# A dilated 3x3 convolution: the first pair stored whole between the halves of the fifth load, and the rows for four DMA engines taken from the second load

## The chip, the core and the metric

The kernel runs on one core of one Trainium2 chip. A core has a matrix engine (PE, with PEld for its weight loads), a vector engine (DVE), a scalar engine (ACT), a general engine (POOL) and a sequencer (SP) that computes nothing and issues the transfers here. Sixteen DMA engines move the data between the device memory (HBM) and the on-chip memory (SBUF). The metric is the device time of one execution in microseconds (us); the median over several executions is compared.

## What is computed

The input `x` has 16 images of 64 channels of 64 x 64 float32 values, `weight` is 128 x 64 x 3 x 3, the dilation is 2, and the output is 16 x 128 x 64 x 64 float32. Cut to what matters:

```python
pad = dilated_k // 2          # 2
x_pad = np.pad(x, ((0, 0), (0, 0), (pad, pad), (pad, pad)), mode='constant')
for b, co, ci, kh, kw in ...:
    output[b, co] += weight[co, ci, kh, kw] * \
        x_pad[b, ci, kh*dilation:kh*dilation+h, kw*dilation:kw*dilation+w]
```

Read once and written once, `x` is 16.8 MB and the output 33.6 MB.

## The kernel before

**Tiling.** Two images make a pair: their 2 x 64 channels fill the 128 partitions, so `x32` of one pair is a tile of 128 partitions by 4096 float32 (16 KB a partition, 2 MiB in all). There are eight pairs (0 to 7). A pair is worked on in four groups of 16 image rows, 32 groups `G` in all; `g` is the group within its pair. The output tile of a pair, `osb`, holds 128 output channels by two images, 32 KB a partition, 4 MiB in all; the two images are stored by separate calls, `store(pb, 0)` and `store(pb, 1)`, 2 MiB each.

**One group.** ACT casts rows of `x32` to float16 (`cast`, line 73), DVE adds pairs of rows (`rowsum`, line 85), PE forms three sets of products in PSUM, `psP`, `psA` and `psB` (line 171), ACT copies `psP` to SBUF as `p_sb` (line 227), and DVE adds `p_sb` to `psA` and to `psB` into the output tile (line 234). A group's last step is the second of these additions. The casts run ahead of the products: after the copy of group 0 three chunks have been cast, and each later group casts two more until it is far enough ahead. Chunks 0 to 3 belong to pair 0, chunks 4 to 7 to pair 1.

**Order.** The schedule is written out by hand: each engine executes its instructions in the order in which the code emits them. Every load and store is issued by SP, on one DMA queue, in program order; a transfer that has to wait for a tile holds up all that SP issues after it.

**Loads.** `x32` has three buffers (`XF = 3`). Pairs 0, 1 and 2 are loaded at the top (lines 89 to 91), pair 0 in two pieces. `load(3)` follows group 0 in the code and waits until the casts have read the whole of pair 0; pair 4 takes the buffer of pair 1 and so waits for chunk 7. In the kernel before, `load(4)` ("the fifth load", `load(XF + 1)`) comes after the stores of group 3. Pairs 5, 6 and 7 are loaded ahead of the stores of pairs 1, 2 and 3 (lines 243 and 244).

**Stores.** Pairs 1 to 6 are stored after their last group, 2 MiB a transfer. Pairs 0 and 7 are stored in halves, after their groups 1 and 3, 1 MiB a transfer. In pair 7 one of these, `store(7, 1)` of the first 32 rows, is cut further: 24 rows of all 128 partitions, and 8 rows (`ROWS4`) in two parts, partitions 0 to 123 and partitions 124 to 127 (`FOUR`). A row of eight image rows is 2 KB in one partition.

```python
FOUR = ((0, P - 4), (P - 4, P))
ROWS4 = 8
```

Of the kernel before, what the change touches and what calls it, by code (L numbers as in the profile page):

```python
# [10 lines left out]
def kernel(  # L11
# [7 lines left out]
    nc = tc.nc  # L19

    B, CI, H, W = x.shape
# [5 lines left out]
    d = 2  # L27

    P = 128
    f32 = mybir.dt.float32  # L30
# [4 lines left out]
    HW = H * W  # L35
    GR = 16
    NG = H // GR
    NBLK = GR // 4
    NH = GR // 2 * W
    npairs = B // 2  # L40
    ngroups = npairs * NG
    chunk_rows = [(g * GR + (d if g else 0), min((g + 1) * GR + d, H)) for g in range(NG)]
    XF = 3

    wpool = ctx.enter_context(tc.tile_pool(name="wpool", bufs=1))
    fpool = ctx.enter_context(tc.tile_pool(name="fpool", bufs=XF))
# [7 lines left out]
    x_pair = x.rearrange("(nb two) c h w -> nb (two c) (h w)", two=2)  # L54
    out_img = out.rearrange("b o h w -> b o (h w)")
# [2 lines left out]

    x32_tiles, x16_tiles, xs_tiles, o_tiles = {}, {}, {}, {}

    def load(pb, cuts=(0, H)):
        x32_tiles[pb] = fpool.tile([P, HW], f32, tag="x32", name="x32")
        for lo, hi in zip(cuts[:-1], cuts[1:]):
            nc.sync.dma_start(
                out=x32_tiles[pb][:, lo * W : hi * W], in_=x_pair[pb, :, lo * W : hi * W]
            )

    def cast(c):
        pb, g = divmod(c, NG)
# [7 lines left out]
    def rowsum(c):  # L77
        pb, g = divmod(c, NG)
        if g == 0:
            xs_tiles[pb] = sxpool.tile([P, HW // 2], f16, tag="xs", name="xs")  # L80
        v = x16_tiles[pb][:, g * GR * W : (g + 1) * GR * W].rearrange(
            "p (b e q) -> p b e q", e=2, q=2 * W
        )
        s = xs_tiles[pb][:, g * NH : (g + 1) * NH].rearrange("p (b q) -> p b q", q=2 * W)
        nc.vector.tensor_tensor(out=s, in0=v[:, :, 0], in1=v[:, :, 1], op=add)  # L85

    w32 = wpool.tile([CO, CI * KH * KW], f32, name="w32")
    nc.sync.dma_start(out=w32, in_=weight.rearrange("o i h w -> o (i h w)"))
    load(0, (0, 2 * GR + d, H))
    load(1)  # L90
    load(2)
    zero = wpool.tile([P, 512], f16, name="zero")
    nc.vector.memset(zero, 0.0)  # L93
# [25 lines left out]
    def turn(k):  # L119
# [24 lines left out]
        out=x16_tiles[0][:, 8 * W : 18 * W], in_=x32_tiles[0][:, 8 * W : 18 * W]  # L144
# [8 lines left out]
    def casts(G):  # L153
        for n in range(2 if G else 3):
            c = ahead[0]
            if c >= ngroups or c > G + (7 if c < 2 * NG else 5):
                return
            cast(c)
            ahead[0] += 1

    def product(ps, src, kind, blk0, nblk, first, last):
        for j in (1, 0, 2):
            dw = (j - 1) * d
            o0, o1 = max(0, -dw), W - max(0, dw)
            t = kind * KW + j
            for hb in range(2):
                pp = slice(hb * CI, (hb + 1) * CI)
                rhs = src(pp, dw + o0, dw + o1)
                po = ps[:, hb * NH + blk0 * 2 * W : hb * NH + (blk0 + nblk) * 2 * W]
                po = po.rearrange("p (r w) -> p r w", w=W)[:, :, o0:o1]  # L170
                nc.tensor.matmul(  # L171
                    out=po,
                    lhsT=w_sb[pp, t * CO : (t + 1) * CO],
                    rhs=rhs,
                    start=first and j == 1,
                    stop=last and j == 2,
                )

    def blocks(x16, b0, n, e):
        v = x16.rearrange("p (b e r w) -> p b e r w", e=2, r=2, w=W)  # L180
        return lambda pp, c0, c1: v[pp, b0 : b0 + n, e, :, c0:c1]

    def store(pb, m, r0=0, r1=H, rows=((0, P),)):
        for lo, hi in rows:
            nc.sync.dma_start(
                out=out_img[2 * pb + m, lo:hi, r0 * W : r1 * W],
                in_=o_tiles[pb][lo:hi, m * HW + r0 * W : m * HW + r1 * W],
            )

    FOUR = ((0, P - 4), (P - 4, P))  # L190
    ROWS4 = 8

    for G in range(ngroups):
        pb, g = divmod(G, NG)
        x16 = x16_tiles[pb]
        xs = xs_tiles[pb].rearrange("p (r w) -> p r w", w=W)
        if g == 0:
            o_tiles[pb] = opool.tile([P, 2 * HW], f32, tag="osb", name="osb")
        o = o_tiles[pb].rearrange("p (m b e q) -> p m b e q", m=2, e=2, q=2 * W)
        b0 = g * NBLK  # L200

        def summed():
            ps = ppool.tile([P, 2 * NH], f32, tag="p", name="psP")
            sv = lambda pp, c0, c1: xs[pp, g * GR // 2 : (g + 1) * GR // 2, c0:c1]
            product(ps, sv, 0, 0, NBLK, True, True)
            return ps

        if G:
            psP = summed()

        psA = apool.tile([P, 2 * NH], f32, tag="ab", name="psA")
        product(psA, blocks(x16, b0, NBLK, 1), 1, 0, NBLK, True, False)
        z = 1 if g == 0 else 0
        product(psA, blocks(x16, b0 + z - 1, NBLK - z, 1), 2, z, NBLK - z, False, True)

        psB = apool.tile([P, 2 * NH], f32, tag="ab", name="psB")
        product(psB, blocks(x16, b0, NBLK, 0), 3, 0, NBLK, True, False)
        z = 1 if g == NG - 1 else 0
        product(psB, blocks(x16, b0 + 1, NBLK - z, 0), 4, 0, NBLK - z, False, True)

        if not G:
            psP = summed()

        if not G:
            casts(0)
        p_sb = spool.tile([P, 2 * NH], f32, tag="psb", name="p_sb")
        nc.scalar.copy(out=p_sb, in_=psP)  # L227
        if G:
            casts(G)
        if G + 1 < ngroups:  # L230
            rowsum(G + 1)
        pv = p_sb.rearrange("p (m b q) -> p m b q", m=2, q=2 * W)
        for e, ps in ((0, psA), (1, psB)):
            nc.vector.tensor_tensor(  # L234
                out=o[:, :, b0 : b0 + NBLK, e],
                in0=ps.rearrange("p (m b q) -> p m b q", m=2, q=2 * W),
                in1=pv,
                op=add,
            )

        if G == 0:
            load(XF)
        if g == NG - 1 and 0 < pb < npairs - XF - 1:
            load(pb + XF + 1)
        if pb in (0, npairs - 1):
            if g % 2 == 1:
                store(pb, 0, (g - 1) * GR, (g + 1) * GR)
                if pb and g == 1:
                    store(pb, 1, 0, 2 * GR - ROWS4)
                    store(pb, 1, 2 * GR - ROWS4, 2 * GR, FOUR)  # L250
                else:
                    store(pb, 1, (g - 1) * GR, (g + 1) * GR)
            if G == NG - 1:
                load(XF + 1)
        elif g == NG - 1:
            store(pb, 0)
            store(pb, 1)

# [34 lines left out]
```

## Time and profile before

| what | value |
|---|---|
| median of 14 executions (lowest to highest) | 126.95 us (126.58 to 127.2) |
| the profiled execution: its own time | 126.99 us |
| its span in the profile | 125.2 us |
| PE busy in the span | 107.0 us (85%) |
| DVE busy | 90.9 us (73%) |
| ACT busy | 65.0 us (52%) |
| bytes moved by DMA | 50.78 MB |

The span is the part of the execution that the profile resolves, from the first to the last recorded instruction; 1.79 us of the profiled execution's own time lie around it. Times in the profile count from the start of the span. In the page's second part the span is cut into 40 slices of 3.13 us, a digit for each: 9 means busy for 90% of the slice or more. The DMA digit is a mean over the sixteen engines. A DMA has a time of issue, when SP executes the instruction, and a time of landing, when its last byte is reported.

### The profile page before, as it was taken

Reading aid. Unit: us, or ns where it says so; the run is one execution under the profiler, and the core shown is the slowest. Engines: PE = TensorE matmul, PEld = TensorE weight load, DVE = VectorE, ACT = ScalarE, POOL = GpSimd, SP = SyncE. Lnnn points to the kernel's source line nnn. Section 1 sums busy time; section 2 is a strip of 40 time slices with the busy share of each in tenths; the row PEclk is TensorE's granted clock in tenths of the full one; section 3 lists DMA queues with packets and bytes.
Section 4 is the critical chain, followed back from the end, with each engine's and each line's share of the span. In section 5 each row is a group of like instructions: output and inputs, shape, how many; then the busy total and the mean of one; then the engine's idle time right before and its main releaser. Section 6 shows DMA issues by size and latency. Waiting matters only on the chain.

```text
span 125.2 us, 2339 instructions
## 1 busy us (share of the span) xinstructions
PE 107.0 (85%) x1000; PEld 57.2 (46%) x1000; DVE 90.9 (73%) x103; ACT 65.0 (52%) x68; POOL 2.2 (2%) x8
## 2 busy tenths in 40 slices
PE   6899699999999999999999999999999999900000
PEld 2344355555555556555555555555555555500000
DVE  0560698988898888988988898889888988740000
ACT  4185798666566656665666566566653333300000
POOL 2400000000000000000000000000000000000000
PEclk9999999999999999999999999999999999995555
DMA  4999999899999999999999999999999999999991
GB/s 114 380 443 440 445 424 408 304 432 427 437 432 434 429 424 424 440 416 419 424 445 427 424 434 419 424 429 440 429 424 434 414 434 429 445 395 416 424 385 55
DMA packets 4466, 50.78 MB, mean 406 GB/s; under 512 B 488, under 2 KB 488, under 8 KB 1000
## 3 DMA queue, kind: packets, MB, share of 16 engines
q1 hardware_dynamic: 4456, 50.63, 96.5%
q8 instruction: 8, 0.13, 0.4%
q14 instruction: 2, 0.02, 0.0%
HBM read 17.07 MB, written 33.55 MB: 404 GB/s over the span
## 4 chain that ended last, share of the span: by engine, by line
PE 82%; DMA 2%; DVE 1%; DVEq 1%; ACT 1%; issue 0%
PE psA L171 32%; PE psB L171 31%; PE psP L171 16%; DMA w<-in_weight_dram 2%; PE wt L124 2%; PE dm L101 2%; DVE osb L234 1%; DVEq L290 1%; ACT p_sb L227 1%; DVE wd L111 0%; DVEq L234 0%
## 5 line engine op out<-in xcount | busy, mean ns | idle before, releaser
L171 PEld LDWEIGHTS <-w_sb 64*128 64x128 f16 x960 | 54.6, 95 | 46.7 <-issue 2.3
L227 ACT COPY p_sb<-psP 128x1024 f32<-128x1024 f32 x32 | 32.4, 1013 | 38.5 <-issue 21.5
L234 DVE TENSOR_TENSOR osb<-psA,p_sb 128x1024 f32<-128x1024 f32 x32 | 39.2, 1225 | 14.8 <-PE psA L171 9.4
L171 PE MATMUL psA<-x,w_sb 64*128 64x496 f16 (+3 forms) x384 | 45.9, 370 | 0.0
L171 PE MATMUL psB<-x,w_sb 64*128 64x496 f16 (+3 forms) x384 | 45.1, 365 | 0.0
L234 DVE TENSOR_TENSOR osb<-psB,p_sb 128x1024 f32<-128x1024 f32 x32 | 39.1, 1222 | 0.0
L73 ACT CAST x<-x 128x1024 f16<-128x1024 f32 (+2 forms) x31 | 32.1, 1046 | 0.0
L171 PE MATMUL psP<-xs,w_sb 64*128 64x496 f16 (+1 forms) x192 | 26.0, 371 | 1.1 <-ACT p_sb L227 1.1
L85 DVE TENSOR_TENSOR xs<-x 128x512 f16<-128x512 f16 x32 | 13.3, 416 | 0.2 <-ACT x L73 0.2
L101 PE MATMUL dm<-zero 128*128 128x512 f16 x10 | 5.0, 622 | 1.2 <-DVE zero L93 1.2
L124 PEld LDWEIGHTS <-wd 128*64 128x64 f16 x30 | 1.5, 162 | 2.5 <-DVE wd L111 1.3
L124 PE MATMUL wt<-ident,wd 128*64 128x128 f16 x30 | 2.2, 314 | 0.4 <-DVE wd L111 0.4
L111 DVE CAST wd<-w 128x192 f16<-128x192 f32 x1 | 0.5, 495 | 2.6 <-DMA w<-in_weight_dram 2.6
L101 PEld LDWEIGHTS <-zero 128*128 128x128 f16 x10 | 1.1, 124 | 2.8 <-issue 1.6
L113 ACT ACT_TABLE_LOAD x1 | 1.3, 1283 | 0.7 <-PEq L276 0.7
L136 ACT CAST w_sb<-wt 128x384 f16<-128x384 f32 x1 | 0.5, 480 | 2.0 <-PE wt L124 2.0
L113 ACT CAST wd<-w 128x192 f16<-128x192 f32 x1 | 0.5, 537 | 1.7 <-DMA w<-in_weight_dram 1.7
L138 DVE CAST w_sb<-wt 128x384 f16<-128x384 f32 x1 | 0.6, 557 | 1.2 <-PE wt L124 1.2
L93 DVE MEMSET zero<- 128x256 uint32 x1 | 0.3, 272 | 0.9 <-PEq L276 0.9
L148 DVE CAST w_sb<-wt 128x384 f16<-128x384 f32 x1 | 0.6, 558 | 0.4 <-PE wt L124 0.4
L112 POOL TENSOR_TENSOR wd<-w 128x192 f16<-128x192 f32 x1 | 0.8, 794 | 2.5 <-DMA w<-in_weight_dram 2.5
L115 POOL CAST wd<-w 128x192 f16<-128x192 f32 x1 | 0.8, 808 | 0.0
(11 smaller groups left out, 3.8 us busy)
## 6 DMA issues: line engine op xcount, KB each, us to landing
out_dram<-osb SPq DMA_DIRECT2D x12, 2048.0 KB, 17.4
x<-in_x_dram SPq DMA_DIRECT2D x7, 2048.0 KB, 15.4
out_dram<-osb SPq DMA_DIRECT2D x7, 1024.0 KB, 11.3
x<-in_x_dram SPq DMA_DIRECT2D x1, 1088.0 KB, 5.5
x<-in_x_dram SPq DMA_DIRECT2D x1, 960.0 KB, 7.3
out_dram<-osb SPq DMA_DIRECT2D x1, 768.0 KB, 14.4
w<-in_weight_dram SPq DMA_DIRECT2D x1, 288.0 KB, 3.0
out_dram<-osb SPq DMA_DIRECT2D x1, 248.0 KB
```

Of the source, the lines that this page charges most:

```text
L73: nc.scalar.copy(out=x16_tiles[pb][:, lo * W : hi * W], in_=x32_tiles[pb][:, lo * W : hi * W])
L85: nc.vector.tensor_tensor(out=s, in0=v[:, :, 0], in1=v[:, :, 1], op=add)
L101: nc.tensor.matmul(out=dm[:, 0:512], lhsT=zero[:, 0:P], rhs=zero)
L112: nc.gpsimd.tensor_tensor(out=wdv[:, 3], in0=wv[:, 0], in1=wv[:, 1], op=sub)
L113: nc.scalar.copy(out=wdv[:, 2], in_=wv[:, 0])
L115: nc.gpsimd.tensor_copy(out=wdv[:, 4], in_=wv[:, 2])
L124: nc.tensor.matmul(out=wts[k % 3][r * CI : (r + 1) * CI, c0 + j * CO : c0 + (j + 1) * CO], lhsT=wd[:, t * CI : (t + 1) * CI], rhs=ident,)
L138: nc.vector.tensor_copy(out=t2[0], in_=t2[1])
L171: nc.tensor.matmul(out=po, lhsT=w_sb[pp, t * CO : (t + 1) * CO], rhs=rhs, start=first and j == 1, stop=last and j == 2,)
L227: nc.scalar.copy(out=p_sb, in_=psP)
L234: nc.vector.tensor_tensor(out=o[:, :, b0 : b0 + NBLK, e], in0=ps.rearrange("p (m b q) -> p m b q", m=2, q=2 * W), in1=pv, op=add,)
L290: with _tile.TileContext(nc) as tc:
```

## The change

Five edits, all in the order and the cutting of transfers; no instruction of PE, DVE, ACT or POOL is changed.

1. Pair 0 is no longer stored in halves: `store(0, 0)` and `store(0, 1)` are issued once, after group 3, 2 MiB each.
2. `load(4)` is cut into two halves of 32 image rows. The first is issued after group 2, ahead of the stores of pair 0, the second after them.
3. `load(1)` is cut into 56 rows of all partitions, and 8 rows in two parts, partitions 0 to 123 and 124 to 127.
4. The store of the first half of image 1 of pair 7 is no longer cut: 1 MiB in one transfer.
5. `load(7)` is cut into two halves, issued one after the other where it stood.

```diff
-    def load(pb, cuts=(0, H)):
-        x32_tiles[pb] = fpool.tile([P, HW], f32, tag="x32", name="x32")
-        for lo, hi in zip(cuts[:-1], cuts[1:]):
...
+    ALL = ((0, P),)
+    FOUR = ((0, P - 4), (P - 4, P))
+    ROWS4 = 8
+
+    def load(pb, *pieces):
+        if pb not in x32_tiles:
+            x32_tiles[pb] = fpool.tile([P, HW], f32, tag="x32", name="x32")
+        for r0, r1, parts in pieces or ((0, H, ALL),):
+            for lo, hi in parts:
+                nc.sync.dma_start(
+                    out=x32_tiles[pb][lo:hi, r0 * W : r1 * W],
+                    in_=x_pair[pb, lo:hi, r0 * W : r1 * W],
+                )
...
-    load(0, (0, 2 * GR + d, H))
-    load(1)
+    load(0, (0, 2 * GR + d, ALL), (2 * GR + d, H, ALL))
+    load(1, (0, H - ROWS4, ALL), (H - ROWS4, H, FOUR))
     load(2)
...
         if G == 0:
             load(XF)
+        if G == NG - 2:
+            load(XF + 1, (0, H // 2, ALL))
         if g == NG - 1 and 0 < pb < npairs - XF - 1:
-            load(pb + XF + 1)
-        if pb in (0, npairs - 1):
+            load(pb + XF + 1, *((0, H, ALL),) if pb < 3 else ((0, H // 2, ALL), (H // 2, H, ALL)))
+        if pb == npairs - 1:
             if g % 2 == 1:
                 store(pb, 0, (g - 1) * GR, (g + 1) * GR)
-                if pb and g == 1:
-                    store(pb, 1, 0, 2 * GR - ROWS4)
-                    store(pb, 1, 2 * GR - ROWS4, 2 * GR, FOUR)
-                else:
-                    store(pb, 1, (g - 1) * GR, (g + 1) * GR)
-            if G == NG - 1:
-                load(XF + 1)
+                store(pb, 1, (g - 1) * GR, (g + 1) * GR)
         elif g == NG - 1:
             store(pb, 0)
             store(pb, 1)
+            if not pb:
+                load(XF + 1, (H // 2, H, ALL))
```

More of the change, by code (lines that the diff above doesn't have):

```diff
@@ L59 @@
     x32_tiles, x16_tiles, xs_tiles, o_tiles = {}, {}, {}, {}
-    def load(pb, cuts=(0, H)):
-        x32_tiles[pb] = fpool.tile([P, HW], f32, tag="x32", name="x32")
-        for lo, hi in zip(cuts[:-1], cuts[1:]):
-            nc.sync.dma_start(
-                out=x32_tiles[pb][:, lo * W : hi * W], in_=x_pair[pb, :, lo * W : hi * W]
-            )
+    ALL = ((0, P),)
[10 more added lines that the diff above has]
+                )
     def cast(c):
@@ L181, in blocks, with store @@
         return lambda pp, c0, c1: v[pp, b0 : b0 + n, e, :, c0:c1]
[L183 to L191, printed above, removed]
+    def store(pb, m, r0=0, r1=H):
+        nc.sync.dma_start(
+            out=out_img[2 * pb + m, :, r0 * W : r1 * W],
+            in_=o_tiles[pb][:, m * HW + r0 * W : m * HW + r1 * W],
+        )
     for G in range(ngroups):
```

## The prediction

> **What bounds the kernel now.** I read first the slices, then the chain of waits with the waits of SP's queue, then windows of the DMA engines at the start and the end.
>
> ```profile
> span 125.2 us, 2339 instructions
> PE   6899699999999999999999999999999999900000
> DMA  4999999899999999999999999999999999999991
> GB/s 114 380 443 440 445 424 408 304 432 427 437 432 434 429 424 424 440 416 419 424 445 427 424 434 419 424 429 440 429 424 434 414 434 429 445 395 416 424 385 55
> ```
>
> PE stops five slices before the end; the DMA engines are full from slice 2 to 39. Only slice 8 falls off in rate, 304 GB/s against 424 to 445.
>
> ```profile
> 109.83 1.13 DVEq L290
> ...
> SPq L290 <- DMA out_dram<-osb: 12.1, 3, 7.5
> ```
>
> The chain of waits ends at 110.96 us, and its 82% of PE misleads: the last 14 us are SP's final wait for stores (12.1 us). So the DMA engines bound the kernel: it ends when the slowest of sixteen has done its share. A faster engine or a shorter compute wait is worth nothing here; a transfer that the DMA engines must wait for, or an uneven share, costs its length on that engine.
>
> ```profile
> 1.50:4.00 2.50, 2.42 (x6) 0.59 (x4) 0.27 (x1) 0.78 (x2) 0.22 (x1) 1.00 0.95 275
> 4.00:21.00 17.00, 15.62 (x136) 7.64 (x138) 11.12 (x16) 11.66 (x15) 1.32 (x2) 1.00 1.01 427
> 21.00:23.50 2.50, 2.50 (x30) 1.39 (x26) 2.09 (x4) 1.79 (x2) 0.00 (x0) 1.00 0.99 292
> 23.50:36.00 12.50, 12.50 (x124) 6.93 (x122) 11.08 (x13) 7.84 (x8) 0.00 (x0) 1.00 1.01 425
> 36.00:61.00 25.00, 25.00 (x246) 13.79 (x242) 22.10 (x25) 15.83 (x17) 0.00 (x0) 1.00 1.01 428
> ...
> 121.00:122.00 1.00, 0.00 (x0) 0.00 (x0) 0.00 (x0) 0.00 (x0) 0.00 (x0) 0.50 0.76 320
> 122.00:123.00 1.00, 0.00 (x0) 0.00 (x0) 0.00 (x0) 0.00 (x0) 0.00 (x0) 0.50 0.39 164
> 123.00:124.00 1.00, 0.00 (x0) 0.00 (x0) 0.00 (x0) 0.00 (x0) 0.00 (x0) 0.50 0.10 41
> ```
>
> The last two numbers of each row are the DMA engines' busy share and their rate. Two losses stand out. From 21.0 to 23.5 us the engines are busy (0.99) but move 292 instead of 427 GB/s: 2.5 x (427 - 292)/427 = 0.79 us lost, on the last packets of the load of pair 3. And the engines end unevenly: 121 to 124 us has shares 0.76, 0.39, 0.10. The trace's completions (one from each engine that carries a part of a DMA) say who ends last: the last store's sixteen come at 120.87 to 122.66 us on ten engines, at 123.26 to 124.09 on five, and at 124.37 on one. The four completions of the 8 KB piece come at 118.50 to 119.31; two further 1 MiB stores of 2.45 us each put these four at 123.4 to 124.2, so they are the group before the last.
>
> **How four engines come in.** The two cut pieces are carried by four engines each, and it is the page that shows it:
>
> ```profile
> DMA packets 4466, 50.78 MB, mean 406 GB/s; under 512 B 488, under 2 KB 488, under 8 KB 1000
> ...
> out_dram<-osb SPq DMA_DIRECT2D x1, 248.0 KB
> out_dram<-osb SPq DMA_DIRECT2D x1, 8.0 KB
> ```
>
> The issues add up to 32 DMAs; 488 tiny packets are 30 x 16 + 2 x 4 completions. So 256 KB go to four engines, 32 rows of 2 KB each, and the completions put their price at 2.49 + 0.19 = 2.68 us per engine. The Trainium skill ("DMA: Bandwidth & Descriptors", Why a DMA increments its semaphore by 16 and not by 1) has the rule: the largest count up to 16 that divides the partitions, 4 for 124, on the lowest-numbered engines; no view here numbers the engines.
>
> **The change part by part.** The sum is made against the profiled execution, 126.99 us (125.2 of span, 1.79 around it), 0.04 over the median.
>
> *Bytes and packets.* Same bytes; 32 DMAs before and after (two stores fewer in pair 0, two fewer pieces in pair 7; two more pieces in load 1, one more in loads 4 and 7 each). Pair 0's 4 MiB go from 8 KB to 16 KB rows, loads 4 and 7 (4 MiB) the other way. The 8 KB stores fill most of 23.5 to 36 us at 425 GB/s, 16 KB rows 36 to 61 at 428: 0.7% of 9.8 us, 0.07 us, gained once and lost once. Sum 0, bounds -0.1 and +0.1. The skill speaks against the cutting (same page, Bandwidth, Measured: batch to at least 1 MiB; Anatomy of one DMA: about 2 us fixed for each). By it two more 1 MiB halves would be some 4 us, an estimate; the rows show no such gap, since transfers queue behind one another.
>
> *Pieces moved to load 1.* Each of the four engines carries its 2.68 us at 13 us instead of at 116 us: on the sum 0 if 2 KB loads run like 2 KB stores. No load of that row length is in the trace; the nearest, the weights' 2.25 KB rows (288 KB, 3.0 us from issue to landing at a cold start), is at 370 GB/s from 2.5 to 3.0 us, near the full rate. Lower bound 0, upper bound twice the price, +2.7 us. I take 0. SP issues two more DMAs here, 0.5 us each: they push load 2 from 2.6 to 3.6 us, hidden since the queue holds work to 13 us. Load 3 is not pushed: it waits for ACT's cast until 10.89. Chunk 7 reads the last rows of pair 1 and is cast at 19.3 us, 3 us after they land (about 16); a cast that waited would hold up the copy of the next group on ACT and with it PE and DVE, whose end at 111 us has 13 us of cover.
>
> *First half of load 4.* SP waits for chunk 7, whose cast ends at 18.42 + 1.89 = 20.3 us. Behind it in SP's queue stand only the stores of pair 0, ready after 24.4. Its issue (0.33 us) is free.
>
> *Stores of pair 0.* Before, 18.45 us was their first issue; now 24.4, when DVE's second addition of group 3 ends (23.16 + 1.22). Will the queue run dry? To 21.0 us it has moved 2.5 x 275 + 17 x 427 = 7.95 MB; the weights, four loads and a half are 9.73 MB; the other 1.78 MB take 4.2 us, to 25.2, and on the twelve engines that do not carry the 2 KB rows 0.6 us less, 24.6. From issue to first packet the weights' load took 1.0 us (0.73 to 1.75; the rate is 6 GB/s before it), so the store arrives at 25.4. The gap is 0.8 us on twelve engines, none if the 0.79 us loss still falls ahead of it. By the skill's figure for the first byte (same page, Latency and other measured facts, about 0.6 us) it would be 0.4 shorter, an estimate. The ten early engines have 124.37 - 122.66 = 1.7 us to spare at the end and hide it; without that spare it costs 0.8. The four and the late one have work then. Sum 0, bounds 0 and +0.8.
>
> *The slow 2.5 us.* No later change from load to store shows it (428 GB/s throughout), so I tie it to the first store, issued 2.5 us before it begins and moving as it ends. Then it stays, and moves to 26 us. What is late next? The engine that finished load 2 at 19.77 us, 1.1 us behind the others (18.18 to 18.69), lost 26.24 - 19.77 - 4.87 = 1.6 us in load 3 (4.87: an undisturbed 2 MiB), the others 0.8. After the change the four engines come 2.1 us later than before to that point and should lose like the late one. Bounds: 0 (as before) and +0.85; nearer to the late engine, +0.6. That puts the four at 124.09 + 0.6 = 124.7, past the 124.37 of the late engine: **+0.3 us**.
>
> *Issues later on.* Load 5 is still issued at 31.8 us by ACT's cast; the queue holds work to 39. Load 7's second issue (0.4 us) delays the stores of pair 3 on SP from 61.5 to 61.9, hidden by a queue that lands load 7 at 72 to 75. In pair 7 SP saves two issues. All 0.
>
> Sum: 126.99 + 0.3 = 127.3, on the median **127.25 us**.
>
> **Rivals.**
> 1. *The loss goes away.* If it came from 1 MiB stores entering behind a running load, the new order has none of that. The late engine gains its 1.6 us and the four some 0.7 (ending at 123.4); then these decide: 124.37 - 123.4 = 1.0 us off, 126.0; with half of the loss left 126.4. For it: the loss is unique, and so was that store's place. Against: its packets were all loads, and something about the first store should stay.
> 2. *The first store is exposed.* If its start needs the whole slow stretch (2.5 us), the queue that runs dry at 24.6 to 25.2 no longer covers it: the stretch becomes an idle of up to 2.5 us instead of a loss of 0.8, +1.0 to +1.7 us on every engine, 128.2. It decides from the moment the idle exceeds 0.8 + 1.7 us on the ten, and at once on the late engine. Against: the weights' cold start took only 1.0 us to the first packet.
> 3. *Nothing moves.* The late engine still ends at 124.37 and the four stay below it: 126.95.
> 4. *2 KB loads are slow.* Twice the price on four engines, 124.1 + 2.7 - 124.37 = +2.4: 129.4.
>
> **How the numbers follow.** No change is what lies within 0.2%, 0.25 us. Forecast 0.36 (126.9 to 127.8, its own range; slower 0.26, same 0.10); loss gone 0.27 (faster 0.26, same 0.01); exposed 0.14, slower; nothing 0.19 (same 0.13, faster 0.04, slower 0.02); slow loads 0.04. Faster 0.30, same 0.24, slower 0.46. The range 126.1 to 128.2 leaves out about a tenth at each end.
>
> **What would show it.** Right: a stretch near 300 GB/s at about 25 to 28 us, none at 21 to 23.5; the four engines last, near 124.7. Rival 1: no such stretch, an end near 123.5. Rival 2: DMA share far under 0.9 around 25 to 28 us. Rival 4: load 3 landing after 29 us. The prediction is wrong if the engines' order at the end is set by something else, such as the late engine's own delays falling elsewhere.

## The result, and the profile after

The changed kernel takes 128.12 us (median of 10, 127.6 to 129.31) against 126.92 (47 executions of the kernel before): the ratio is 1.0104, 95% interval 1.0088 to 1.012. It is slower by 1.2 to 1.3 us. A second measurement (experiment 1) gave 127.97 us and 1.0081 (1.0066 to 1.0096). Ratios, and the medians of the changed kernels, leave out executions more than 1.5% above the fastest of the same kernel; the first profile of the changed kernel is of such a one (span 127.8 us), so what follows is read from the second, of 127.88 us, which is 0.89 us over the profiled execution before.

Its slices, and the waits of SP's queue:

```profile
span 126.1 us, 2340 instructions
DMA  4999999999999999999999999999999999999981
GB/s 141 367 451 411 288 333 431 418 444 426 416 424 442 429 437 426 418 431 431 431 431 392 434 452 424 431 416 431 442 426 416 437 416 447 426 408 426 426 374 55
...
SPq L291 <- DMA out_dram<-osb: 14.6, 5, 5.0
```

The end is still SP's wait for the last stores. The fall in rate is no longer in slice 8 (304 GB/s before) but in slices 5 and 6 (288 and 333). Windows of the same profile; the last two numbers are the DMA engines' share and rate:

```profile
1.50:4.00 2.50, 2.42 (x6) 0.60 (x4) 0.42 (x2) 0.93 (x2) 0.37 (x1) 1.00 0.92 278
4.00:12.00 8.00, 6.07 (x68) 3.21 (x70) 3.82 (x9) 5.33 (x8) 1.18 (x2) 1.00 1.01 422
12.00:17.00 5.00, 5.00 (x50) 2.67 (x48) 5.00 (x6) 4.25 (x5) 0.00 (x0) 1.00 1.06 294
17.00:21.00 4.00, 4.00 (x42) 2.21 (x40) 3.49 (x5) 2.67 (x3) 0.00 (x0) 1.00 0.98 414
21.00:23.50 2.50, 2.50 (x30) 1.43 (x28) 1.96 (x3) 1.06 (x2) 0.00 (x0) 1.00 1.01 433
23.50:36.00 12.50, 12.24 (x120) 6.67 (x118) 10.78 (x13) 9.02 (x11) 0.00 (x0) 1.00 1.00 426
36.00:61.00 25.00, 25.00 (x246) 13.79 (x242) 22.18 (x25) 15.92 (x17) 0.00 (x0) 1.00 1.01 428
121.00:122.00 1.00, 0.00 (x0) 0.00 (x0) 0.00 (x0) 0.00 (x0) 0.00 (x0) 0.50 0.89 377
122.00:123.00 1.00, 0.00 (x0) 0.00 (x0) 0.00 (x0) 0.00 (x0) 0.00 (x0) 0.50 0.70 295
123.00:124.00 1.00, 0.00 (x0) 0.00 (x0) 0.00 (x0) 0.00 (x0) 0.00 (x0) 0.50 0.29 123
124.00:125.00 1.00, 0.00 (x0) 0.00 (x0) 0.00 (x0) 0.00 (x0) 0.00 (x0) 0.50 0.08 33
```

From 12 to 17 us the engines are busy and move 294 GB/s: 5 x (427 - 294)/427 = 1.56 us lost. In exchange the stretch at 21 to 23.5 us is gone (433 in place of 292 GB/s), 0.79 us won. The difference, 0.77 us, is nearly the whole result: the mean of the last store's sixteen completions went from 122.62 to 123.47 us (+0.85), the last of them from 124.37 to 125.26 (+0.89). All sixteen engines end later, not four.

The stretch is the time in which four engines load the 2 KB rows (their packets start from 12.5 to 16.8 us; the two pieces complete at 17.0 to 17.9) while twelve load pair 2. A packet is one piece of a transfer that one engine moves, here one row of one partition. The trace's packets show both kinds slowed: between 13.5 and 16.5 us the median 2 KB packet takes 150 ns and the median 16 KB packet 1149 ns; undisturbed they take 84 and 611.

### The profile page after: what moved, and what is told of

Its sections match the earlier page's. It is cut to its first block, busy times and chain, and to the rows that moved or that the text cites. A ratio compares the mean times of both kernels' runs of the same rounds, so it can differ in the third digit from the quotient of the medians.

```text
span 127.8 us, 2340 instructions
## 1 busy us (share of the span) xinstructions
PE 105.7 (83%) x1000; PEld 54.8 (43%) x1000; DVE 90.3 (71%) x103; ACT 65.0 (51%) x68; POOL 2.3 (2%) x8
## 4 chain that ended last, share of the span: by engine, by line
PE 64%; DVE 2%; DVEq 1%; issue 0%
PE psB L178 25%; PE psA L178 25%; PE psP L178 14%; DVE osb L237 2%; DVEq L291 1%; DVEq L237 0%
## 5 line engine op out<-in xcount | busy, mean ns | idle before, releaser
L178 PEld LDWEIGHTS <-w_sb 64*128 64x128 f16 x960 | 52.7, 94 | 49.4 <-issue 3.2
L178 PE MATMUL psA<-x,w_sb 64*128 64x496 f16 (+3 forms) x384 | 45.0, 365 | 0.0
L131 PE MATMUL wt<-ident,wd 128*64 128x128 f16 x30 | 1.6, 244 | 0.4 <-DVE wd L118 0.4
L145 DVE CAST w_sb<-wt 128x384 f16<-128x384 f32 x1 | 0.6, 559 | 0.9 <-PE wt L131 0.9
L121 DVE TENSOR_TENSOR wd<-w 128x192 f16<-128x192 f32 x1 | 0.8, 787 | 0.0
```

What stands on the lines that cost most here:

```text
L121: nc.vector.tensor_tensor(out=wdv[:, 1], in0=wv[:, 2], in1=wv[:, 1], op=sub)
L131: nc.tensor.matmul(out=wts[k % 3][r * CI : (r + 1) * CI, c0 + j * CO : c0 + (j + 1) * CO], lhsT=wd[:, t * CI : (t + 1) * CI], rhs=ident,)
L178: nc.tensor.matmul(out=po, lhsT=w_sb[pp, t * CO : (t + 1) * CO], rhs=rhs, start=first and j == 1, stop=last and j == 2,)
```

## The experiments

Two theories at first: the moved rows do it, or the new order, whose loads run longer without a store between them.

**1. The changed kernel once more.**

> The changed kernel once more, unedited, for a second profile of it, since times ran from 127.6 to 129.31 us and the one profile (span 127.8) is among the longest. Both theories expect about 128.1. Theory Rows (the 2 KB pieces of load 1 on four engines slow all sixteen): the slow stretch begins at 12.7 us again, with 16 KB packets at 1.0 to 1.1 us while the 2 KB packets last. Theory Reads (an unbroken run of loads falls to about 360 GB/s after some 20 us): the stretch begins at 19 to 21 us in this profile and lasts until the stores start; then the early start of the first profile was the extreme case.

127.97 us, 1.0081 (1.0066 to 1.0096); the profile is the one above. The stretch begins and ends with the 2 KB rows again, with no fall at 19 to 21 us: for the rows, against the length of the run of loads.

**2. The new order alone**, against the changed kernel; measured twice, the second time more often.

```diff
-    load(1, (0, H - ROWS4, ALL), (H - ROWS4, H, FOUR))
+    load(1)
...
-            load(pb + XF + 1, *((0, H, ALL),) if pb < 3 else ((0, H // 2, ALL), (H // 2, H, ALL)))
+            load(pb + XF + 1)
...
+                if g == 1:
+                    store(pb, 1, 0, 2 * GR - ROWS4)
+                    store(pb, 1, 2 * GR - ROWS4, 2 * GR, FOUR)
...
```

> Only the new order: pair 0 stored whole between the halves of load 4; load 1 and load 7 whole, the cut of pair 7's store as before the change. Theory Rows: 126.7 to 127.2, rate near 427 GB/s to 21 us. Theory Reads: the loads run unbroken to about 26 us, so the slow stretch (292 GB/s from 21.0 to 23.5 us before the change) goes on until the stores start, 1 to 1.3 us lost in place of 0.8 and more on single engines: 127.8 to 128.3.

> The new order alone once more, more rounds: its ten times of the first job lay in two groups, 126.4 to 126.7 and 127.8 to 128.6. If the order is worth something by itself the fast group again lies 0.3 us or more under the kernel before; if it is worth nothing the median is within 0.25 us of it.

First 126.66 us (median of seven), ratio 0.9994 (0.9957 to 1.0031); then 126.67 us (median of eleven), ratio 0.9954 (0.9917 to 0.9992). The order costs nothing: its medians lie 0.3 us under the 126.98 of the kernel before both times, though only the second ratio is clear of 1. Windows of the second profile:

```profile
12.00:17.00 5.00, 5.00 (x50) 2.64 (x49) 5.00 (x6) 4.09 (x5) 0.00 (x0) 1.00 1.01 429
21.00:23.50 2.50, 2.50 (x30) 1.49 (x28) 2.33 (x4) 1.55 (x3) 0.00 (x0) 1.00 0.94 400
24.00:26.00 2.00, 2.00 (x24) 1.06 (x20) 2.00 (x3) 0.94 (x2) 0.00 (x0) 1.00 1.04 434
41.00:43.50 2.50, 2.50 (x28) 1.34 (x24) 2.09 (x4) 1.55 (x2) 0.00 (x0) 1.00 1.02 341
```

No fall at 12 to 17 us, none where the first store comes in (24 to 26), and a smaller one in the load of pair 5: 2.5 x (428 - 341)/428 = 0.51 us. So the first store does not bring the stretch with it.

**3. The moved rows alone**, in the old order: load 1 cut and pair 7's store uncut. The edit is shown against the kernel before.

```diff
-    load(1)
+    load(1, (0, H - ROWS4, ALL), (H - ROWS4, H, FOUR))
...
-                if pb and g == 1:
-                    store(pb, 1, 0, 2 * GR - ROWS4)
-                    store(pb, 1, 2 * GR - ROWS4, 2 * GR, FOUR)
-                else:
-                    store(pb, 1, (g - 1) * GR, (g + 1) * GR)
+                store(pb, 1, (g - 1) * GR, (g + 1) * GR)
```

> Only the moved rows: load 1 cut into 56 rows, 124 and 4 partitions of 8 rows, pair 7's store uncut, order of the kernel before. Theory Rows: the stretch begins at 12.7 us as in the changed kernel, 127.8 to 128.5. Theory Reads: the stores still break the loads at the same place, so 126.8 to 127.2 and 427 GB/s from 4 to 20 us.

127.83 us, 1.0077 (1.0052 to 1.0103): the rows alone make the loss of experiment 1. Two windows of it:

```profile
12.00:17.00 5.00, 5.00 (x50) 2.64 (x49) 5.00 (x6) 4.09 (x5) 0.00 (x0) 1.00 1.03 306
21.00:23.50 2.50, 2.50 (x30) 1.49 (x28) 2.12 (x3) 1.18 (x2) 0.00 (x0) 1.00 0.99 426
```

Here the old order stands, with 1 MiB stores of pair 0 behind the load of pair 3, and the stretch at 21 to 23.5 us is gone all the same. So it went with the moved rows, not with the order; why, these runs don't show.

**4. The same cut, all sixteen engines**, against the changed kernel.

```diff
-    load(1, (0, H - ROWS4, ALL), (H - ROWS4, H, FOUR))
+    load(1, (0, H - ROWS4, ALL), (H - ROWS4, H, ALL))
```

> The changed kernel with the 8 rows of load 1 loaded by one DMA on all 128 partitions (2 KB rows still, sixteen engines; nothing evens out the end by four engines any more, which costs about 0.6 us on the other twelve). Theory Rows: without the four uneven engines no stretch at 12.7 us; 427 GB/s to 20 us, time 126.9 to 127.5. Theory Reads: 128 to 128.7, the stretch from about 20 us to the first store.

127.15 us, 1.0021 (0.9998 to 1.0044). The window of the lost stretch in its profile:

```profile
12.00:17.00 5.00, 4.76 (x46) 2.61 (x47) 4.78 (x5) 3.94 (x5) 0.00 (x0) 1.00 1.03 433
```

2 KB rows as such, loaded by all sixteen engines, cost nothing that these runs resolve.

**5. The kernel before once more.**

> The kernel before once more, unedited: where does its slow stretch (21.0 to 23.5 us, 0.79 us) fall in a second profile? If it belongs to the first store or to the load of pair 3: again at 21 to 24 us, in that load. If it is an event that each execution has at a time of its own (0.8 us at 42 us in the profiles of both kernels with the new order and no rows on four engines): at another time, of the same size.

126.78 us in one execution, and the stretch in the same window of its profile:

```profile
21.00:23.50 2.50, 2.50 (x30) 1.47 (x26) 2.33 (x4) 1.78 (x3) 0.00 (x0) 1.00 0.94 301
```

Here the first store was issued at 16.97 us, 1.5 us earlier than in the first profile (18.45), and the stretch did not move with it. So the issue of the store does not set it.

**6. The same bytes on four engines, in long rows**, with the bytes of the other twelve unchanged; against the changed kernel.

```diff
-    load(1, (0, H - ROWS4, ALL), (H - ROWS4, H, FOUR))
+    SIXTEEN = ((0, P - 16), (P - 16, P - 12), (P - 12, P - 8), (P - 8, P - 4), (P - 4, P))
+    load(1, (0, H, SIXTEEN))
```

> The changed kernel with the same 256 KB of load 1 given to the same four engines, but in whole rows: partitions 0 to 111 by one DMA, and four DMAs of 4 partitions with 16 KB rows (4 packets of 16 KB an engine in place of 32 of 2 KB). Theory Small (short packets of four engines amid other loads slow all sixteen): no stretch at 13 to 17 us, 126.4 to 127.2. Theory Four (any piece on four engines amid loads does it, long rows too): the stretch stays, 250 to 370 GB/s at 13 to 17 us, 127.7 to 128.3.

138.49 us, 1.0882 (1.0795 to 1.0968): far more than either theory allowed. Windows of its profile, first while the DMA of 112 partitions runs, then while the four small pieces do:

```profile
9.00:13.00 4.00, 2.48 (x26) 1.27 (x23) 0.42 (x1) 2.30 (x3) 0.00 (x0) 1.00 1.04 270
15.00:21.00 6.00, 5.62 (x54) 2.86 (x51) 4.37 (x6) 0.97 (x1) 0.00 (x0) 1.00 1.03 158
```

**8. Sixteen rows in place of eight**, against the changed kernel.

```diff
-    ROWS4 = 8
+    ROWS4 = 16
```

> The changed kernel with 16 rows in place of 8 in the cut of load 1 (4 KB rows, 512 KB on the four engines, 32 packets each as before). The end is uneven by it, so read the stretch: if the slowing goes with the count of short packets, it lasts as long as the 32 packets do and costs the others no more per us; at full rate these 32 packets take 5.0 us in place of 2.7. Theory Small: a smaller fall in rate than to 253 GB/s, since the packets are twice as long. Theory Four: the same fall to about 250 to 265 GB/s for about twice the time, 7 to 8 us; time 130 to 131.

134.68 us (1.0618, 1.0593 to 1.0643). The window of its pieces:

```profile
14.00:22.00 8.00, 8.00 (x80) 4.32 (x78) 6.92 (x9) 3.77 (x4) 0.00 (x0) 1.00 1.04 260
```

So it is not the short packet: long rows fall to 158 GB/s, and 4 KB rows to 260 GB/s for 8 us, much as the 2 KB rows do for half as long (267 GB/s from 13 to 17 us in the changed kernel). (The times also hold an uneven end and, in 6, compute waiting for late loads; the rates are what count.) In 6 the pieces of four partitions sit in sixteen neighbouring partitions, and the 112 partitions are cut by seven an engine in place of eight; that DMA, on sixteen engines alike, is slow already (270 GB/s). That pointed at where the data is written.

**9. Even shares, other partitions.** Load 1 as two DMAs of 64 partitions and load 2 as four of 32, from the new order alone.

```diff
-    load(1)
-    load(2)
+    load(1, (0, H, ((0, 64), (64, P))))
+    load(2, (0, H, ((0, 32), (32, 64), (64, 96), (96, P))))
```

> The new order alone with load 1 as two DMAs of 64 partitions and load 2 as four of 32: all sixteen engines have the same share, but engine e writes other partitions than in a DMA of 128 (4 neighbouring ones, then 2). Theory Partitions (the slowing comes from engines that write into a group of partitions that another engine also writes): load 1 runs at about half rate, 200 to 260 GB/s from 9 to 18 us, load 2 still slower; time 130 or more. Theory Uneven (it takes four engines that are out of step with twelve): 420 to 435 GB/s from 9 to 21 us, time 126.5 to 127.3.

137.13 us (1.0763, 1.0675 to 1.0851). Windows over the two loads:

```profile
9.00:18.00 9.00, 7.31 (x70) 3.83 (x68) 5.30 (x7) 3.81 (x4) 0.00 (x0) 1.00 0.99 209
18.00:27.00 9.00, 5.43 (x42) 2.48 (x38) 3.76 (x4) 5.70 (x6) 0.00 (x0) 0.81 1.00 209
```

All sixteen engines are busy with equal shares and move 209 GB/s: the median 16 KB packet of load 1 takes 1284 ns, 2.1 times 611. Four engines out of step with twelve are not needed. Nor is it the size of a DMA: the 256 KB over all 128 partitions in experiment 4 ran at full rate. What is left is where an engine writes, or at what distance the engines read.

**13 and 14. SBUF side or HBM side.** Both start from the order alone. Number 13 loads pair 1 by eight DMAs of 16 partitions whose source rows are 128 KB apart, as the engines' rows are in a DMA of 128 if each engine takes eight neighbouring rows; the channels of pair 1 come out permuted. Number 14 keeps one DMA of 128 partitions but starts its source rows 8 KB apart, so that all distances in HBM are halved (64 KB between neighbouring engines by the same assumption, as in load 1 of experiment 9); pair 1 gets other values. No view shows which rows an engine takes.

```diff
+    far = x_pair[1].rearrange("(e t) f -> t e f", t=8)
+    for t in range(8):
+        nc.sync.dma_start(out=x32_tiles[1][16 * t : 16 * t + 16, :], in_=far[t])
```

```diff
+    one = x_pair[1]
+    close = bass.AP(one.tensor, one.offset, [[HW // 2, P], [1, HW]])
+    nc.sync.dma_start(out=x32_tiles[1], in_=close)
```

> The new order alone with load 1 as eight DMAs of 16 partitions, whose rows in HBM lie as far apart as the sixteen engines' rows do in a DMA of 128 (128 KB), so that each engine reads where it always reads but writes into partitions of others (the channels of pair 1 come out in another order). Theory SBUF (engines that write into a shared group of partitions): half rate while load 1 runs, 200 to 260 GB/s from about 9 to 18 us, 2.1 times the 611 ns of a 16 KB packet or more. Theory HBM (engines that read at a smaller distance than 128 KB): 420 to 435 GB/s.

> The new order alone with load 1 as one DMA of 128 partitions, whose rows start 8 KB apart in HBM and overlap, so that neighbouring engines read 64 KB apart as in the pieces of 64 partitions, but each writes its usual partitions (pair 1 gets other values). Theory SBUF: 420 to 435 GB/s, 611 ns a packet, 126.4 to 127.0 or the slower group. Theory HBM: about 1284 ns a packet, 210 to 250 GB/s from 9 to 18 us.

One execution each: 140.91 and 126.46 us. Windows over load 1, first of 13, then of 14:

```profile
10.00:21.00 11.00, 7.04 (x53) 3.14 (x50) 5.23 (x6) 3.81 (x4) 0.00 (x0) 0.84 0.97 134
```

```profile
9.00:18.00 9.00, 7.69 (x74) 3.96 (x72) 6.16 (x8) 7.88 (x9) 0.00 (x0) 1.00 1.02 433
```

In 13 the median 16 KB packet takes 1860 ns, 3.0 times as long; in 14, with half the distance in HBM, it takes 611. Halving every distance in HBM doesn't slow a load over all 128 partitions, and rows 128 KB apart don't save one over 16. So it is the SBUF side: among other loads, loads ran at full rate as DMAs over all 128 partitions, and slowed down as DMAs over 112, 64, 32 or 16 of them, or beside a piece that only four engines load. Which partitions get in one another's way is not shown.

**7, 10 and 12. The same pieces beside other traffic.** Number 7 cuts load 5 (the twelve engines then store pair 1), 12 the first half of load 4 (they then store pair 0), 10 the second store of pair 1 (four engines store, twelve load pair 6). Load 1 is whole in all three; 7 and 12 are the changed kernel otherwise, 10 the order alone with pair 7's store uncut.

```diff
+    LATER = {
+        1: ((0, H - ROWS4, ALL), (H - ROWS4, H, FOUR)),
...
+            load(pb + XF + 1, *LATER[pb])
```

```diff
+            load(XF + 1, (0, H // 2 - ROWS4, ALL), (H // 2 - ROWS4, H // 2, FOUR))
```

```diff
+            if pb == 1:
+                store(pb, 1, 0, H - ROWS4)
+                store(pb, 1, H - ROWS4, H, FOUR)
```

> The changed kernel with the cut moved from load 1 to load 5, whose last pieces are followed on the queue by the stores of pair 1: the four engines read 2 KB rows while the other twelve store. If short loads only hurt beside other loads: no stretch around 39 to 48 us, 126.4 to 127.2. If short loads on four engines hurt whatever the others do: a stretch of some 4 us near 43 us, about 1.0 us lost, 127.7 to 128.3.

> The changed kernel with the rows for four engines taken from the first half of load 4 in place of load 1: that half is the last load ahead of the stores of pair 0, so four engines load while twelve store, which cost nothing in load 5. Expected if the neighbour on the queue decides: no stretch at 12 to 17 us nor at 24 to 29, time as with the order alone, 126.4 to 127.3. If rows for four engines in any load cost 1 us: 127.7 to 128.3.

> The new order alone, with the cut of pair 7's store moved to the second store of pair 1, which load 6 follows on the queue: four engines store 2 KB rows while twelve load. If only writes into SBUF meet one another: no stretch around 53 to 60 us, 126.4 to 127.3. If four engines beside loading ones always slow them: under 300 GB/s for some 4 us there, 127.5 to 128.3.

Windows while the pieces run, of 7, 12 and 10 in this order:

```profile
44.00:46.50 2.50, 2.50 (x26) 1.36 (x24) 2.43 (x3) 1.18 (x3) 0.00 (x0) 1.00 1.03 415
```

```profile
25.00:28.00 3.00, 3.00 (x32) 1.64 (x30) 2.59 (x4) 1.96 (x2) 0.00 (x0) 1.00 1.03 427
```

```profile
52.00:56.00 4.00, 4.00 (x42) 2.16 (x38) 3.58 (x5) 1.85 (x2) 0.00 (x0) 1.00 1.04 413
```

In all three the median 2 KB packet takes 84 ns and the median 16 KB packet 611, and the rates stay at 413 GB/s or more: no such slowing. The kernel before is the fourth case, four engines storing beside twelve that store, at 427 GB/s:

```profile
115.00:119.00 4.00, 0.00 (x0) 0.00 (x0) 0.00 (x0) 0.00 (x0) 0.00 (x0) 0.50 1.03 427
```

Of the four combinations only loads beside loads slow one another here; both write into SBUF. The times, though, were not what I expected of them: 127.89 us for 7 (1.0074, 1.003 to 1.0119), 127.55 for 10 (1.0037, 1.0001 to 1.0072) and 127.79 for 12 (median of three; 1.0114, 1.0034 to 1.0195), none better than the order alone. They spread widely, from 126.92 to 128.81 us in 7, but even their lowest (126.92, 127.04 and 127.5) lie above the lowest of the order alone (126.4). In 7 the load of pair 5 has a longer slow stretch ahead of the pieces:

```profile
40.00:43.00 3.00, 3.00 (x32) 1.61 (x30) 2.59 (x4) 1.78 (x3) 0.00 (x0) 1.00 0.98 291
```

In the profile of 12 (127.5 us, the shortest of its times) the completions' mean is that of the kernel before (122.67 against 122.62 us), but the last four engines end at 124.2 to 124.8. Why these kernels are slower although their pieces run at full speed is open.

## Why the prediction was wrong

The sign was right and 128.12 us lies in the range, 0.08 us from its upper end. But the forecast was +0.3 us and the change cost 1.2 to 1.3, by a mechanism that the sum has no term for; what was forecast to make it slower did not happen. So the sign was luck.

- **The bound** was right: the last completion sets the end in every profile, compute ends long before it. (The slices were read loosely: besides slice 8 the full ones run from 380 to 445 GB/s, not from 424. Nothing rests on it.)
- **Pieces moved to load 1: this step failed.** It took the cost on the sum as 0 and bounded it by the packets' own duration on four engines. The step asked how fast a 2 KB load runs by itself (in experiments 7 and 12, beside stores, 84 ns a packet, as I took it), not what it does to the twelve engines that load beside it. Measured: 150 ns for the 2 KB packets and 1149 for the 16 KB ones over some 4 us, 1.56 us lost on the mean of all sixteen; 0.79 of it came back because the slow 2.5 us went away. The loss of the twelve is missing from the sum, not mis-sized.
- **The slow 2.5 us** was tied to the first store, and wrongly: experiment 5 moved the store's issue and not the stretch, with the order alone nothing falls at 24 to 26 us, and experiment 3 has the old order and stores and no stretch there. The +0.3 us built on it, four engines losing more there, never occurred; the profile of 127.88 us has no slow stretch after 17 us, and its four late engines complete load 2 at 21.94 to 22.42 us and load 3 at 26.77 to 27.25, 4.83 us apart, undisturbed.
- **Stores of pair 0**: no gap, and none was charged. The reckoning itself used an issue at 24.4 us; the changed kernel issues at 22.66, because compute ran 1.5 us late in the profile I read: the first copy of `psP` begins at 12.42 us there, at 10.95 in experiment 5.
- **Bytes, packets, first half of load 4, later issues**, all put at 0: nothing in experiments 2 and 4 contradicts it.
- **Rivals.** The loss going away had a part of truth: with the order alone the stretch shrinks from 0.79 to 0.51 us, and the time by 0.46% (0.08 to 0.83) in one of two measurements, but not for the reason given: experiment 3 keeps the 1 MiB stores behind a load and has no stretch. The exposed first store did not occur: in the profile of 127.88 us the first half of load 4 completes at 26.68 us on its first engine and the first store behind it at 31.59, 4.91 us later, about one undisturbed 2 MiB. Slow 2 KB loads named the right transfer and nearly its price (150 for 84 ns), but not the other victims: all sixteen engines end later, and load 3 landed at 27.25 us, not after 29.

## What to carry to other kernels

A transfer that goes to few engines must be priced by what it does to the transfers beside it, not by its own length: here 256 KB on four engines slowed 16 KB loads of twelve others from 611 to 1149 ns. Among other loads, loads ran at full rate here only as DMAs over all 128 partitions, so cut them by rows and not by partitions; the uneven pieces of the kernel before, among stores, ran at 427 GB/s, so if four engines are to carry more, let them carry it there. And where the engines are busy but the rate is low, look first at which other transfers are in flight, before tying it to whatever was issued shortly before.

## What was not expected of the hardware

- Loads by DMAs of 64 or 32 partitions ran at 209 GB/s, of 112 at 270, of 16 at 134, of 128 at 433, with 16 KB rows in each. The Trainium skill ("DMA: Bandwidth & Descriptors", Rules for kernel authors) says of two transfers to disjoint partition halves not to bother, since they share the engines and serialize; here two halves take twice as long as one DMA of 128, which is more than sharing. The same page (Specifications) gives eight partitions an engine as a convention and sixteen SBUF ports; that the ports are what is shared fits, but no run here shows a port.
- The kernel before in both profiles, the order alone, and experiments 4 and 14, all with loads over 128 partitions throughout, hold a further slow stretch at the end of one 2 MiB load: pair 3's in the old order (292 and 301 GB/s from 21 to 23.5 us), pair 5's in the new (341 in the second profile of experiment 2). With the four engines' rows in load 1 it is missing, in either order. Neither the first store nor its issue sets it; its cause stays open.
